# A masked softmax whose first half tile is loaded as two transfers, 16 partitions and 112

## The chip, the core and the metric

The kernel runs on one core of a Trainium2 chip. The metric is device time in microseconds (us) of one execution; lower is better. Engines are named as in the profile: DVE is VectorE, ACT is ScalarE, POOL is GpSimd, PE is TensorE, and SP is SyncE, which here only issues transfers.

## What is computed

A softmax over the last axis, of which only the first `lengths[b]` columns count; the other columns of the output are zero.

```python
x: (16, 8, 256, 256) float32;  lengths: 16 whole numbers from 128 to 255
for b in range(batch):
    masked = x[b, :, :, :lengths[b]]
    masked = masked - np.max(masked, axis=-1, keepdims=True)
    exp_masked = np.exp(masked)
    result[b, :, :, :lengths[b]] = exp_masked / np.sum(exp_masked, axis=-1, keepdims=True)
```

## The kernel before, in words

One batch is 2048 rows of 256 numbers, 2 MB. It is laid on 128 partitions with 16 rows each (`nt` = 16), so a partition holds 16 KB of a batch, and half a tile (`half` = 8 rows a partition) is 1 MB, or 8 KB a partition. Eight such tiles (`slots`) lie in the on-chip buffer `xt`. The 16 batches go through them in the order that `batch_of` gives; the first is batch 1.

For each batch: a load; a mask on VectorE (`mask`, `clip`, L248), which pulls the columns past the length far down; the exponential on ScalarE, as one instruction for the first four rows of a partition (L374) and one for each further row with its sum taken along (L377); on VectorE the sum of the first four rows (`total`, L269), then for each half a reciprocal (L279) and a multiplication (`divide`, L282); a store. The largest element is not subtracted. A check at the end (L317 to L328) finds whether any sum left the safe range, and only then a second, safe version runs.

Loads come from three queues. ScalarE's queue loads the lengths (L142). SP's queue loads the first tile in two halves (L145), each with a semaphore of its own, `s_ld[0]` and `s_ld[1]`:

```python
for h in range(2):
    s = slice(h * half, (h + 1) * half)
    nc.sync.dma_start(out=xt[:, 0, s], in_=x_f[batch_of(0), :, s]).then_inc(s_ld[h], 16)
```

POOL's queue loads the next three tiles whole (L196), after it has filled part of a later slot with zeros and has waited for `s_v`; the remaining twelve are loaded in a loop (L168), each only as wide as its length needs, in steps of 8 columns from 160, and each after an earlier load has landed and an earlier store has freed the slot.

Behind its two loads SP issues all stores (L154), in pieces of a quarter tile to a whole one (`parts`). Each waits for the multiplication that made its data (`s_out`), and up to the thirteenth tile also for the store two tiles before (L153).

VectorE masks the first tile in two halves. `mask(0, first half)` waits until `s_ld[0]` is 16, `mask(0, second half)` until `s_ld[1]` is 16. Every other mask treats a whole tile. After these two, VectorE's order is written out by hand: divide the first half, mask the next tile, divide the second half, sum the next tile's first rows.

Of the kernel before, what the change touches and what calls it, by code (L numbers as in the profile page):

```python
# [21 lines left out]
def kernel(  # L22
# [6 lines left out]
    nc = tc.nc  # L29
    P = nc.NUM_PARTITIONS  # L30
# [5 lines left out]
    half = nt // 2  # L36
# [3 lines left out]
    x_f = x.rearrange("b h q k -> b (h q) k").rearrange("b (p t) k -> b p t k", p=P)  # L40
# [9 lines left out]
    def batch_of(pos):  # L50
        return pos + 1 if pos < ahead - 1 else {ahead - 1: 15, 15: 0}.get(pos, pos)
# [22 lines left out]
    xt = pool.tile([P, slots, nt, seq_k], F32, name="xt")  # L74
# [31 lines left out]
    with tc.tile_critical(no_gpsimd_drain=True):  # L106
# [4 lines left out]
        s_ld = [sem(f"s_ld{k}") for k in range(3)]  # L111
# [28 lines left out]


        nc.scalar.dma_start(out=word64, in_=lengths[None, :]).then_inc(s_word, 16)  # L142
        for h in range(2):
            s = slice(h * half, (h + 1) * half)
            nc.sync.dma_start(out=xt[:, 0, s], in_=x_f[batch_of(0), :, s]).then_inc(s_ld[h], 16)  # L145
        for b in range(batch):
            s_b = s_st[b % 2] if b < late else s_late if b < batch - 1 else s_last
            for s in parts(b):
# [3 lines left out]
                if 2 <= b < late and s.start == 0:  # L152
                    nc.sync.wait_ge(s_b, 64 * (b // 2 + 2))  # L153
                nc.sync.dma_start(  # L154
                    out=out_f[batch_of(b), :, s, :], in_=xt[:, b % slots, s, :]
# [67 lines left out]
        def step(ins):  # L223
# [8 lines left out]
                out=down, in0=iota_i, scalar1=0.5, scalar2=-big, op0=ALU.add, op1=ALU.mult  # L232
# [7 lines left out]
                out=len_s, in0=len_f, scalar1=big, scalar2=None, op0=ALU.mult  # L240
# [4 lines left out]
        def clip(b, s, lo, hi):  # L245

            t = xt[:, b % slots, s, lo:hi]
            return nc.vector.scalar_tensor_tensor(  # L248
                out=t,
                in0=down[:, None, lo:hi].to_broadcast([P, s.stop - s.start, hi - lo]),  # L250
                scalar=len_s[:, batch_of(b) : batch_of(b) + 1],
                in1=t,
                op0=ALU.add,
                op1=ALU.min,
            )

        def mask(b, s):
            if b == 0:
                nc.vector.wait_ge(s_ld[s.start // half], 16)
            elif b == ahead - 1:  # L260
                nc.vector.wait_ge(s_ld[2], 16)
            else:
                par = (b - 1 if b < ahead else b) % 2
                nc.vector.wait_ge(s_sw[par], 16 * max(b // 2, 1))
            clip(b, s, mid, seq_k).then_inc(s_min, 1)
# [10 lines left out]
        def divide(b, h):  # L276
# [10 lines left out]
            ).then_inc(s_out, 1)  # L287

        mask(0, slice(0, half))
        mask(0, slice(half, nt))  # L290
        total(0)
        for b in range(batch):


            first = b != 1
            if first:
                divide(b, 0)
            if b + 1 < batch:
                mask(b + 1, slice(0, nt))
            if not first:  # L300
                divide(b, 0)
            divide(b, 1)
            if b + 1 < batch:
                total(b + 1)
# [14 lines left out]
        for k, (_, _, edge, op) in enumerate(checks):  # L319
            nc.vector.tensor_scalar(  # L320
                out=bad[:, k : k + 1],
# [13 lines left out]
        with nc.vector.Else():  # L335
            with nc.Fori(0, batch, 1, engines=[DVE]) as i:
                nc.vector.wait_ge(g_ld, 16 * i + 16)
                nc.vector.scalar_tensor_tensor(
                    out=g_t,
# [8 lines left out]
                    out=neg_max, in_=g_t, op=ALU.max, axis=AX, negate=True  # L348
# [5 lines left out]
                    out=g_t,  # L354
# [10 lines left out]
        with nc.Fori(0, batch // slots, 1, engines=[ACT]) as turn:  # L365
            for slot in range(slots):
                for h in range(2):
# [7 lines left out]
                    for j in range(h * half + lump * (1 - h), (h + 1) * half):  # L375
                        e = xt[:, slot, j, :]
                        ins = nc.scalar.activation(  # L377
                            out=e, in_=e, func=EXP, accum_out=row_sum[:, slot, j : j + 1]
# [5 lines left out]
        with nc.scalar.If(a_redo >= 1):  # L384
# [4 lines left out]
            with nc.Fori(0, batch, 1, engines=[ACT]) as i:  # L389
                nc.scalar.dma_start(out=g_t, in_=x_g[:, bass.ds(i, 1)]).then_inc(g_ld, 16)  # L390
                nc.scalar.wait_ge(g_v, 3 * i + 2)
                with nc.Fori(0, nt, 1, engines=[ACT]) as t:
                    e = g_t[:, bass.ds(t, 1), :]
                    nc.scalar.activation(
                        out=e,
                        in_=e,
# [41 lines left out]
```

## Time and profile before

| What | Value |
|---|---|
| Time, median of 3 runs (lowest to highest) | 154.69 us (154.58 to 154.70) |
| Span of the profiled execution, first to last instruction | 152.8 us |
| VectorE busy | 134.6 us |
| ScalarE busy | 95.1 us |
| GpSimd busy | 21.3 us |
| Read from and written to main memory | 27.98 MB and 33.55 MB |
| Mean rate of all transfers over the span | 403 GB/s |
| First-half and second-half load, issue to landing (median of the two) | 6.4 us |

How to read it: the profile is of one execution and its span is a little shorter than the time of a run, which also covers what lies before the first and after the last instruction. A window row gives, for a stretch of the span, the length, then busy time and number of instructions of PE, PEld, DVE, ACT and POOL, the clock granted to TensorE, the mean busy share of the 16 DMA engines and their GB/s. A packet is counted in the stretch in which it starts, with its whole length and duration, so a share can pass 1. A timeline row gives start, duration, engine, line, operation, tiles, and in brackets how long the engine was idle before and who released it; "SPq" and "POOLq" are issues of transfers.

### The profile page before, as it was taken

The numbers are of one execution on the slowest core, as the hardware profiler recorded it, in microseconds if no ns is written. First come the engines' busy times: TensorE is split into PE (matmuls) and PEld (weight loads), VectorE is DVE, ScalarE is ACT, GpSimd is POOL, SyncE is SP. The second block draws the span as 40 slices with busy tenths as digits, with TensorE's granted clock in tenths as the row PEclk, the third lists the DMA queues.
The fourth block names the chain that finished last, engine by engine and source line by source line (L and its number), as shares of the span: only waits on it lengthen the run. The fifth ranks groups of instructions, "written<-read, shape, count | busy, mean of one in ns | idle before, by whom it ended". The sixth has DMA issues, their size and how long they took to land.

```text
span 152.8 us, 818 instructions
## 1 busy us (share of the span) xinstructions
PE 0.3 (0%) x2; PEld 0.2 (0%) x2; DVE 134.6 (88%) x107; ACT 95.1 (62%) x402; POOL 21.3 (14%) x29
## 2 busy tenths in 40 slices
PE   0000000000000000000000000000000000000000
PEld 0000000000000000000000000000000000000000
DVE  1369999999999999999999999999999999999500
ACT  3096699339394967859393939577593939395000
POOL 4962110030303020030300220302000000000000
DMA  4999999999999999999999999999999999999994
GB/s 107 420 446 433 401 435 347 421 445 420 394 397 422 405 421 411 411 409 405 419 411 418 408 399 419 408 410 423 417 421 419 413 420 422 435 435 442 429 410 187
DMA packets 10646, 61.57 MB, mean 403 GB/s; under 512 B 898, under 2 KB 1010, under 8 KB 7058
## 3 DMA queue, kind: packets, MB, share of 16 engines
q1 hardware_dynamic: 5904, 35.65, 56.7%
q0 software_dynamic: 4736, 25.89, 41.9%
q14 instruction: 4, 0.03, 0.1%
q10 hardware_dynamic: 2, 0.00, 0.0%
HBM read 27.98 MB, written 33.55 MB: 403 GB/s over the span
## 4 chain that ended last, share of the span: by engine, by line
DVE 87%; DMA 5%; issue 1%; SPq 0%; PE 0%
DVE xt L282 48%; DVE xt L248 23%; DVE row_sum L269 12%; DMA xt<-in_x_dram 5%; DVE inv_sum L279 3%; DVE ends L317 0%; SPq L145 0%; DVE bad L320 0%; PE count L218 0%; DVE redo L328 0%; SPq L433 0%; SPq L106 0%
## 5 line engine op out<-in xcount | busy, mean ns | idle before, releaser
L377 ACT ACTIVATE xt<-xt 128x256 f32<-128x256 f32 x192 | 76.6, 400 | 0.2 <-DVE xt L248 0.2
L282 DVE TENSOR_TENSOR xt<-xt,inv_sum 128x2048 f32<-128x2048 f32 x32 | 73.3, 2292 | 1.1
L374 ACT ACTIVATE xt<-xt 128x1024 f32<-128x1024 f32 x16 | 16.9, 1056 | 42.8 <-DVE xt L248 42.8
L248 DVE SCALAR_TENSOR_TENSOR xt<-down,len_s,xt 128x2048 f32<-128x2048 f32 (+1 forms) x17 | 37.7, 2219 | 5.0 <-DMA xt<-in_x_dram 5.0
L377 ACT ACTIVATION_READ_ACCUMULATOR xt<-xt 128x1 f32 x192 | 35.9, 187 | 0.0
L168 POOL DMA_DIRECT2D xt<-in_x_dram x12 | 13.2, 1104 | 84.0 <-DMA xt<-in_x_dram 62.3
L269 DVE TENSOR_REDUCE row_sum<-xt 128x4 f32<-128x1024 f32 x16 | 19.4, 1210 | 0.0
L279 DVE RECIPROCAL inv_sum<-row_sum 128x8 f32<-128x8 f32 x32 | 6.3, 198 | 0.5
L191 POOL MEMSET xt<- 128x1536 f32 x4 | 5.4, 1398 | 1.1 <-DVE len_s L239 1.1
L361 ACT ACT_TABLE_LOAD x1 | 1.3, 1283 | 1.6 <-SPq L106 1.6
L196 POOL DMA_DIRECT2D xt<-in_x_dram x3 | 1.8, 590 | 0.0
L231 DVE TENSOR_SCALAR down<-iota_i 128x256 f32<-128x256 int32 x1 | 0.3, 300 | 1.6 <-POOL iota_i L181 1.6
L317 DVE TENSOR_REDUCE ends<-inv_sum 128x1 f32<-128x256 f32 x2 | 0.7, 408 | 0.0
L236 DVE CAST len_b<-word 1x16 bf16<-1x16 int32 x1 | 0.2, 164 | 0.4 <-DMA word<-in_lengths_dram 0.4
L239 DVE TENSOR_SCALAR len_s<-len_f 128x16 f32<-128x16 f32 x1 | 0.2, 176 | 0.3 <-PE len_f L216 0.3
L218 PE MATMUL count<-bad,ones_c 128*1 128x3 bf16 x1 | 0.2, 165 | 140.8 <-DVE bad L320 140.8
L181 POOL IOTA iota_i<- 128x256 int32 x1 | 0.3, 331 | 0.6 <-SPq L106 0.6
L328 DVE TENSOR_REDUCE redo<-count 1x1 f32<-1x3 f32 x1 | 0.1, 150 | 0.3 <-PE count L218 0.3
L320 DVE TENSOR_SCALAR bad<-ends 128x1 bf16<-128x1 f32 x3 | 0.3, 150 | 0.0
L187 POOL MEMSET seed<- 1x1 f32 x2 | 0.2, 225 | 0.0
L218 PEld LDWEIGHTS count<-bad,ones_c 128*1 128x1 bf16 x1 | 0.1, 79 | 140.8 <-DVE bad L320 140.8
L361 ACT ACTIVATE warm<-const-float32-0.0 128x1 f32<-128x1 f32 x1 | 0.2, 204 | 0.0
(10 smaller groups left out, 1.1 us busy)
## 6 DMA issues: line engine op xcount, KB each, us to landing
out_dram<-xt SPq DMA_DIRECT2D x20, 1024.0 KB
xt<-in_x_dram POOLq DMA_DIRECT2D x4, 2048.0 KB, 16.3
out_dram<-xt SPq DMA_DIRECT2D x15, 512.0 KB
xt<-in_x_dram POOLq DMA_DIRECT2D x3, 1728.0 KB, 16.7
out_dram<-xt SPq DMA_DIRECT2D x2, 2048.0 KB
xt<-in_x_dram POOLq DMA_DIRECT2D x2, 1600.0 KB, 16.0
xt<-in_x_dram POOLq DMA_DIRECT2D x2, 1280.0 KB, 14.7
xt<-in_x_dram SPq DMA_DIRECT2D x2, 1024.0 KB, 6.4
```

Source lines behind the costliest of these rows:

```text
L168: nc.gpsimd.dma_start(out=xt[:, slot, :, :w], in_=x_n[:, b, :, :w]).then_inc(s_sw[par], 16)
L191: nc.gpsimd.memset(xt[:, b, :, low:], 0.0).then_inc(s_fill, 1)
L196: nc.gpsimd.dma_start(out=xt[:, b], in_=x_f[batch_of(b)]).then_inc(s_sw[b - 1] if b < 3 else s_ld[2], 16)
L218: nc.tensor.matmul(count, lhsT=ones_c, rhs=bad, start=True, stop=True).then_inc(s_count, 1)
L248: return nc.vector.scalar_tensor_tensor(out=t, in0=down[:, None, lo:hi].to_broadcast([P, s.stop - s.start, hi - lo]), scalar=len_s[:, batc ...
L269: nc.vector.tensor_reduce(out=row_sum[:, b % slots, :lump], in_=xt[:, b % slots, :lump, :], op=ALU.add, axis=AX,).then_inc(s_exp[0], 1)
L279: step(nc.vector.reciprocal(out=inv_sum[:, b, s], in_=row_sum[:, b % slots, s]))
L282: nc.vector.tensor_tensor(out=t, in0=t, in1=inv_sum[:, b, s, None].to_broadcast([P, half, seq_k]), op=ALU.mult,).then_inc(s_out, 1)
L317: step(nc.vector.tensor_reduce(out=ends[:, k : k + 1], in_=values, op=op, axis=AX))
L361: nc.scalar.activation(out=warm, in_=nc.const_aps.tensor(0.0, (P, 1), F32), func=EXP)
L374: nc.scalar.activation(out=e, in_=e, func=EXP).then_inc(s_lump, 1)
L377: ins = nc.scalar.activation(out=e, in_=e, func=EXP, accum_out=row_sum[:, slot, j : j + 1])
```

## The change

The first half of the first tile is loaded as two transfers on SP's queue, one after the other: partitions 0 to 15, then partitions 16 to 127. The second half is still one transfer of all partitions, now the third on the queue. Both pieces of the first half count on `s_ld[0]`, and the first mask waits until it is 32. All lines below move down by one.

```diff
-        for h in range(2):
+        edge = 16
+        for h, p in ((0, slice(0, edge)), (0, slice(edge, P)), (1, slice(0, P))):
             s = slice(h * half, (h + 1) * half)
-            nc.sync.dma_start(out=xt[:, 0, s], in_=x_f[batch_of(0), :, s]).then_inc(s_ld[h], 16)
+            nc.sync.dma_start(out=xt[p, 0, s], in_=x_f[batch_of(0), p, s]).then_inc(s_ld[h], 16)
...
             if b == 0:
-                nc.vector.wait_ge(s_ld[s.start // half], 16)
+                nc.vector.wait_ge(s_ld[s.start // half], 16 * (2 - s.start // half))
```

## The prediction

> **What bounds the kernel now.** I read the page's head and its slices first, then the chain that ended last, then the timeline at both ends, then busy time by window.
>
> ```profile
> span 152.8 us, 818 instructions
> PE 0.3 (0%) x2; PEld 0.2 (0%) x2; DVE 134.6 (88%) x107; ACT 95.1 (62%) x402; POOL 21.3 (14%) x29
> ...
> DMA  4999999999999999999999999999999999999994
> GB/s 107 420 446 433 401 435 347 421 445 420 394 397 422 405 421 411 411 409 405 419 411 418 408 399 419 408 410 423 417 421 419 413 420 422 435 435 442 429 410 187
> ...
> DVE 87%; DMA 5%; issue 1%; SPq 0%; PE 0%
> ```
>
> Two things look full: VectorE (DVE, 88%) and the 16 DMA engines (a 9 in every slice but the first and last). The chain names VectorE for 87%. It is followed back from the last instruction of an engine, though, and stores still run after that. The end of the timeline and the windows around it decide:
>
> ```profile
> 142.46 0.36 SPq L154 DMA_DIRECT2D out_dram<-xt  x1
> ...
> 143.74 0.15 DVE L328 TENSOR_REDUCE redo<-count 1x1 f32<-1x3 f32 x1 [0.26 <-PE count L218]
> ```
> ```profile
> 10.00:20.00 10.00, 0.00 (x0) 0.00 (x0) 9.90 (x9) 7.20 (x33) 1.84 (x3) 1.00 1.02 427
> 20.00:24.00 4.00, 0.00 (x0) 0.00 (x0) 3.96 (x4) 4.00 (x16) 0.03 (x1) 1.00 0.92 370
> 24.00:60.00 36.00, 0.00 (x0) 0.00 (x0) 35.55 (x27) 23.37 (x101) 4.63 (x4) 1.00 1.02 413
> 60.00:100.00 40.00, 0.00 (x0) 0.00 (x0) 39.52 (x29) 27.60 (x122) 5.76 (x5) 1.00 1.02 410
> 100.00:140.00 40.00, 0.00 (x0) 0.00 (x0) 39.48 (x31) 29.23 (x125) 1.15 (x1) 1.00 1.02 422
> ...
> 142.50:150.00 7.50, 0.17 (x1) 0.08 (x1) 1.10 (x7) 0.00 (x0) 0.00 (x0) 1.00 0.98 418
> 150.00:152.80 2.80, 0.00 (x0) 0.00 (x0) 0.00 (x0) 0.00 (x0) 0.00 (x0) 1.00 0.26 108
> ```
>
> The last two columns are the mean busy share of the DMA engines and GB/s. The last store is issued at 142.46 and VectorE is through at 143.89, yet 418 x 7.5 + 108 x 2.8 = 3.4 MB still go out after 142.5. The last store is only 1 MB of that: the engines have a backlog of over 2 MB, and have been at a share of about 1.0 since 10 us. So the end is set by the DMA engines: when they start, how fast they are in the first microseconds, and then 61 MB at their pace. VectorE is some 7 us ahead at the end. A gap in the engines at the start is not made up later; one in VectorE is.
>
> The start, in detail:
>
> ```profile
> 1.14 0.86 SPq L145 DMA_DIRECT2D xt<-in_x_dram  x2
> ...
> 4.37 1.76 POOL L196 DMA_DIRECT2D xt<-in_x_dram  x3
> ...
> 6.46 1.28 DVE L248 SCALAR_TENSOR_TENSOR xt<-down,len_s,xt 128x1024 f32<-128x1024 f32 x1 [3.47 <-DMA xt<-in_x_dram]
> ...
> 9.26 1.29 DVE L248 SCALAR_TENSOR_TENSOR xt<-down,len_s,xt 128x1024 f32<-128x1024 f32 x1 [1.52 <-DMA xt<-in_x_dram]
> ...
> 14.27 10.95 SPq L154 DMA_DIRECT2D out_dram<-xt  x5
> ```
> ```profile
> 0.00:2.00 2.00, 0.00 (x0) 0.00 (x0) 0.30 (x1) 0.35 (x1) 0.92 (x10) 1.00 0.00 0
> 2.00:3.00 1.00, 0.17 (x1) 0.10 (x1) 0.34 (x2) 0.99 (x2) 0.00 (x0) 1.00 0.95 172
> 3.00:4.00 1.00, 0.00 (x0) 0.00 (x0) 0.00 (x0) 0.14 (x1) 0.95 (x1) 1.00 0.91 319
> 4.00:5.00 1.00, 0.00 (x0) 0.00 (x0) 0.00 (x0) 0.00 (x0) 1.00 (x2) 1.00 0.95 401
> 5.00:6.00 1.00, 0.00 (x0) 0.00 (x0) 0.00 (x0) 0.00 (x0) 1.00 (x3) 1.00 1.00 418
> ```
>
> Nothing moves before 2 us. Against the 427 GB/s of 10 to 20 us, the three microseconds from 2 to 5 lose (255 + 108 + 26) / 427 = 0.91 us. That is the most that a better start could give back.
>
> **The change, part by part.** It adds one transfer on SP's queue, and cuts the first 1 MB (128 rows of 8 KB) into 16 rows and 112 rows. Of compute instructions nothing is added or moved; the first mask waits for both pieces on one semaphore.
>
> *One more issue on SP.* Two issues take 0.86 us, so 0.43 each. The 112 rows are issued 0.43 later than the whole was begun, at about 1.57, and the second half at about 2.0 instead of 1.57. The second half hides: the engines need 8 packets each of the first half before it, and that work lasts beyond 5 us. Behind it on SP stands the first store, which is issued at 14.27 because it waits for VectorE. POOL's loads (4.37) and ScalarE's load of the lengths stand on other queues, and neither is moved. Cost 0; if that cover were gone, 0.43.
>
> *The first packets.* Two windows give the price of one 8 KB packet on one engine:
>
> ```profile
> DMA packets 14, 0.11 MB, mean 209 GB/s; under 512 B 0, under 2 KB 0, under 8 KB 0
> ...
> q1 hardware_dynamic: 14, 0.11, 136.1%
> ```
> ```profile
> DMA packets 24, 0.20 MB, mean 393 GB/s; under 512 B 0, under 2 KB 0, under 8 KB 0
> ...
> q1 hardware_dynamic: 24, 0.20, 92.7%
> ```
>
> The first window is 2.05 to 2.6 us: 1.361 x 16 engines x 0.55 us / 14 packets = 0.86 us each. The second is 4.6 to 5.1: 0.927 x 16 x 0.5 / 24 = 0.309 us each. The engines do not start together:
>
> ```profile
> 2.00:2.20 0.20, 0.00 (x0) 0.00 (x0) 0.00 (x0) 0.20 (x1) 0.00 (x0) 1.00 0.68 123
> 2.20:2.40 0.20, 0.00 (x0) 0.00 (x0) 0.09 (x1) 0.20 (x1) 0.00 (x0) 1.00 2.41 328
> 2.40:2.60 0.20, 0.00 (x0) 0.01 (x1) 0.07 (x1) 0.20 (x1) 0.00 (x0) 1.00 0.66 123
> 2.60:2.80 0.20, 0.17 (x1) 0.09 (x1) 0.00 (x0) 0.20 (x1) 0.00 (x0) 1.00 0.35 123
> ```
>
> GB/s x 0.2 us / 8.192 KB counts the packets that start in each row: 3, 8, 3 and 3. So 16 engines take up their first packet over some 0.6 us, on average near 2.35. If the spread is the time in which 128 rows are described, 16 rows are described in an eighth of it, all engines start near 2.2, and their next packets (issued at 1.57, so due 0.43 after the present times, 2.6 to 3.2) are there when a 0.86 us packet ends. That gives 2.35 - 2.2 = 0.15 us per engine, 0.55 for the last engine; if the spread has another cause, nothing. I take 0.15.
>
> *Where these packets write.* In the present load the 16 engines work at the same time on rows spread over all 128 partitions. In the first piece all 16 first packets go to 16 neighbouring partitions, and come from one stretch of x. No row of the trace has such a transfer. If the engines then share their way into the memory by n, each first packet has (n - 1) x 0.309 more: 0 for n = 1, 0.31 for two, 0.93 for four, 2.2 for eight, and 15 x 0.309 = 4.6 us for all sixteen, which is the far end. The nearest row (24 packets at 0.309 each, 128 partitions) is n = 1; but it owes that pace to its spread, and a sixteenth of the partitions at no loss would mean that any place takes the pace of all 16. I take the middle of the five steps, n = 4: +0.93.
>
> The Trainium skill, "SBUF — State Buffer", section "Door 1: The DMA port swizzle", speaks against the change: partitions 0 to 15 reach 4 of the 16 DMA ports, and a transfer to them was measured there at 104 GB/s. By that page 128 KB would take 1.26 us instead of the 0.31 of a full-width packet, an estimate of +0.95, and the sum would come out the same; no run here shows it yet.
>
> *The 112 rows.* Each engine has 7 rows instead of 8. If shares are neighbouring rows, 7 do not line up with the 8 that each engine has in every other transfer, so now and then two engines meet in one place, in the 112 rows and where a late engine still writes them while the next transfer begins. Nothing in the trace shows it: 0 if they never meet, two packets (0.62) if a quarter of the seven meet another's; I take 0.2, nearer to the row of undisturbed packets.
>
> *After that.* VectorE's first two masks start after waits on these loads (6.46 and 9.26), so its whole row shifts by about the same 1 us. That is covered by its 7 us at the end. The thinnest place of the DMA row is 20 to 24 (share 0.92); stores come 1 us later there, but loads are queued, so I cost it at 0. If that cover fails it costs up to the same 1 us once more.
>
> **Sum:** 0.93 - 0.15 + 0.2 = +0.98, say +1.0 us. The profiled span is 152.8; the median of the runs, 154.69, is 1.9 above it, for what lies around the span. So a span of 153.8, and 152.8 + 1.0 + 1.9 = **155.7 us**. With two sharing it is 0.31 - 0.15 + 0.2 = +0.4, with four, the full 0.62 and nothing won at the start +1.55: the forecast's own range is 155.1 to 156.3.
>
> **The rivals.**
>
> *Faster: the engines start together.* No sharing (n = 1), shares that do not meet, and the spread of first packets is gone. For it: 0.6 us of spread, first packets of 0.86 us that would cover the gap to the second issue, and an end set by the last engine. It decides if the last engine to start is also the last to end: 0.15 on average, 0.55 for the last, in the middle 0.35: 154.3 us. Against it: 16 engines on 16 partitions must cost nothing.
>
> *No change.* The first data come when the memory answers, whenever a packet is taken up: the early packets take 0.86 us and so end together with later ones. Then starting earlier only lengthens the first packet: 154.7. This is also the case in which the change does not do what it says. The Trainium skill, "DMA: Bandwidth & Descriptors", section "Rules for kernel authors", says of two transfers to disjoint partition halves "Don't bother", since both spray over the same 16 engines; that would be this rival, and the full DMA row agrees that there is no free engine to win.
>
> *Slower by another way: engines belong to partitions.* If an engine serves fixed rows, 16 rows wake only two to four engines and the others wait for the second issue, 0.43 later than now. No packet is slowed, but most engines start 0.43 later, and with an end set by the last one that is +0.43: 155.1. The same page, section "Why a DMA increments its semaphore by 16 and not by 1", has 16 and 112 rows both split over 16 engines, which speaks against it; no run here shows it.
>
> **How the numbers follow.** Chances: the forecast 0.55, engines by partition 0.13, no change 0.14, start together 0.18. Something within 0.2% (0.31 us) is about what a measurement of this kernel cannot tell from no change. Faster by more: 0.14 of the rival's 0.18 and nothing else. Within: the 0.14 of no change, the rival's other 0.04, and 0.04 of engines by partition, 0.22. Slower: 0.55 and 0.09, 0.64. The range leaves out the far sharing (eight or sixteen, about 0.1) above and the largest gain below: 154.3 to 156.3.
>
> **What would show it.** In the changed profile SP has three issues of 0.43, about 1.3 us together. If the engines start together, all 16 first packets start before 2.4. If they share, packets that start before 2.6 take 1.2 us or more rather than 0.86, the rows from 2 to 5 lose about 1.9 us instead of 0.91, the first mask starts near 7.4 and the second near 10.2, and the tail after 142.5 is longer by 1 us while rows from 24 to 140 keep 410 to 422 GB/s. If engines belong to partitions, few packets start before 2.6 and each takes no longer. The forecast is wrong if the first packets take 0.9 us or less, or if the loss at the start grows and the end does not follow, which would mean that the end is not set by the DMA engines.

## The result

The changed kernel takes 155.62 us (median of 10 runs) against 154.61 for the kernel before (10 runs): 1.0071 times, interval 1.0052 to 1.0090. It is slower by 1.0 us (1.1 by the ratio), as forecast, and 155.62 stands beside the forecast of 155.7. The profile and the runs below say that two of the forecast's terms had the wrong size, though, and that their errors cancelled: the number was met by luck.

The profiled execution of the changed kernel took 156.72 us, 1.1 above the median, so a second profile (155.74 us, span 154.1) is drawn on below wherever the size matters. First the head of the page, after:

```profile
span 155.1 us, 819 instructions
...
DMA  4999999999999999999999999999999999999991
GB/s 91 285 431 444 427 424 382 417 434 427 397 390 423 407 417 415 414 411 401 417 414 412 410 408 415 409 410 421 418 423 417 419 419 425 427 444 439 408 429 59
```

At the start the first two slices differ most (91 and 285 GB/s where there were 107 and 420); the last one is lower too (59 where there was 187). The windows of the start, after; the last two columns are the DMA engines' busy share and GB/s:

```profile
2.00:2.20 0.20, 0.00 (x0) 0.00 (x0) 0.00 (x0) 0.20 (x1) 0.00 (x0) 1.00 0.45 164
2.20:2.40 0.20, 0.00 (x0) 0.00 (x0) 0.10 (x1) 0.20 (x1) 0.00 (x0) 1.00 1.86 492
2.40:2.60 0.20, 0.00 (x0) 0.02 (x1) 0.06 (x1) 0.20 (x1) 0.00 (x0) 1.00 0.02 0
```
```profile
2.00:3.00 1.00, 0.17 (x1) 0.10 (x1) 0.34 (x2) 0.99 (x2) 0.00 (x0) 1.00 1.28 238
3.00:4.00 1.00, 0.00 (x0) 0.00 (x0) 0.00 (x0) 0.14 (x1) 0.95 (x1) 1.00 0.60 156
4.00:5.00 1.00, 0.00 (x0) 0.00 (x0) 0.00 (x0) 0.00 (x0) 1.00 (x2) 1.00 0.91 328
5.00:6.00 1.00, 0.00 (x0) 0.00 (x0) 0.00 (x0) 0.00 (x0) 1.00 (x3) 1.00 1.02 295
6.00:7.00 1.00, 0.00 (x0) 0.00 (x0) 0.00 (x0) 0.00 (x0) 1.00 (x2) 1.00 1.04 246
7.00:8.00 1.00, 0.00 (x0) 0.00 (x0) 0.00 (x0) 0.00 (x0) 1.00 (x2) 1.00 0.93 295
```

164 x 0.2 / 8.192 = 4 packets start before 2.2 us and 12 before 2.4: all 16 engines have begun, sooner than before. Then no packet of 8 KB starts for 0.2 us. From 4 to 8 the engines are nearly always busy (0.91 to 1.04) but move only 246 to 328 GB/s, where before they moved 401 to 475. So packets do not wait there; they take longer. Share x 16 us / packets gives 0.36 us a packet in the row from 4 to 5 and 0.41 to 0.56 in the three behind it, instead of 0.309. All of these packets are still on SP's queue. The first 1 MB is through near 6.1 us by the sum of the rows, so the slow packets last into the second half, which is loaded at full width.

The price of the first packets themselves, and of those behind them, after, from 2.05 to 2.4 us and from 2.6 to 3.0:

```profile
DMA packets 16, 0.13 MB, mean 374 GB/s; under 512 B 0, under 2 KB 0, under 8 KB 0
...
q1 hardware_dynamic: 16, 0.13, 132.0%
```
```profile
DMA packets 21, 0.11 MB, mean 266 GB/s; under 512 B 8, under 2 KB 8, under 8 KB 8
...
q1 hardware_dynamic: 21, 0.11, 202.8%
```

The narrow piece's 16 packets take 1.320 x 16 x 0.35 / 16 = 0.46 us each (0.51 in the second profile). The 13 packets of the 112 rows behind them take 2.028 x 16 x 0.4 / 13 = 1.0 us each.

A measure for all kernels here is the time lost from 2 to 8 us: the sum of (427 - GB/s) / 427 over its six rows. Before it is 0.80 us; after, 2.35, and 2.20 in the second profile. That is 1.4 to 1.55 more, of which 1.0 is in the median time. Of the first profile's 1.55, only 0.40 falls from 2 to 5 us, where the forecast had it, and 1.15 from 5 to 8.

The rest of the run, after:

```profile
1.14 1.33 SPq L146 DMA_DIRECT2D xt<-in_x_dram  x3
...
8.52 1.28 DVE L249 SCALAR_TENSOR_TENSOR xt<-down,len_s,xt 128x1024 f32<-128x1024 f32 x1 [5.53 <-DMA xt<-in_x_dram]
12.48 1.28 DVE L249 SCALAR_TENSOR_TENSOR xt<-down,len_s,xt 128x1024 f32<-128x1024 f32 x1 [2.67 <-DMA xt<-in_x_dram]
```
```profile
24.00:60.00 36.00, 0.00 (x0) 0.00 (x0) 35.55 (x27) 24.95 (x108) 4.63 (x4) 1.00 1.01 410
60.00:100.00 40.00, 0.00 (x0) 0.00 (x0) 39.48 (x30) 28.20 (x120) 4.80 (x5) 1.00 1.02 411
100.00:140.00 40.00, 0.00 (x0) 0.00 (x0) 39.55 (x29) 27.25 (x116) 2.10 (x2) 1.00 1.02 423
```
```profile
143.38 2.29 DVE L283 TENSOR_TENSOR xt<-xt,inv_sum 128x2048 f32<-128x2048 f32 x1
```

Three issues of 0.44; the second mask starts 3.2 us later than before (12.48 against 9.26) and VectorE's last multiplication ends 3.2 later (145.67 against 142.44). The time grew by 1.0 only. The transfer rows from 24 to 140 are the same as before, within 3 GB/s.

### The profile page after: what moved, and what is told of

It is laid out like the page before. It is cut to its first block, busy times and chain, and to the rows that moved or that the text cites. A ratio compares the mean times of both kernels' runs of the same rounds, so it can differ in the third digit from the quotient of the medians.

```text
span 155.1 us, 819 instructions
## 1 busy us (share of the span) xinstructions
PE 0.3 (0%) x2; PEld 0.2 (0%) x2; DVE 134.7 (87%) x107; ACT 95.1 (61%) x402; POOL 21.3 (14%) x29
## 4 chain that ended last, share of the span: by engine, by line
DVE 86%; DMA 7%; issue 1%; SPq 1%; PE 0%
DVE xt L283 47%; DVE xt L249 23%; DVE row_sum L270 12%; DMA xt<-in_x_dram 7%; DVE inv_sum L280 3%; SPq L146 1%; DVE ends L318 0%; DVE bad L321 0%; PE count L219 0%; DVE redo L329 0%; SPq L434 0%; SPq L106 0%
```

## The experiments

Three theories at first: **A**, the forecast's, that the narrow piece is itself slow; **B**, that the 112 rows are, as their shares do not line up; **C**, that any third transfer at the start costs its issue. All ratios are to the kernel before, and a difference in us is its ratio's excess over 1 times the 154.6 us of that kernel; by this measure the change is +1.1.

**An extra narrow load ahead of two whole halves.** Edit:

```diff
+        nc.sync.dma_start(out=extra[0:16], in_=x_f[batch_of(0), 0:16, :half]).then_inc(s_extra, 16)
         for h in range(2):
```

> The kernel before, with one more load ahead of its first half: the same 16 rows of 8 KB as the change's first piece, to partitions 0 to 15 of a buffer that nothing reads. The two half loads stay whole. In every theory the 16 packets take 0.31 us of each engine. Theory A (the narrow piece is itself slow, four engines to a way): 0.31 + 0.93 - 0.15 = +1.1 us against before. Theory B (the 112 rows are what is slow, because their shares do not line up): +0.2 to +0.4. Theory C (a third transfer at the start costs its issue, whatever it holds): 0.31 + 0.43 = +0.7.

Measured: 155.08 us, 1.0031 (1.0019 to 1.0043), so +0.48, of which 0.31 are the bytes that it adds. Net +0.17: A's 0.93 is refuted and C's +0.7 is just outside the interval (+0.29 to +0.66), which B's +0.2 to +0.4 overlaps. Its transfers in the window from 2.05 to 2.4 us, and from 2.5 to 3.0:

```profile
DMA packets 16, 0.13 MB, mean 374 GB/s; under 512 B 0, under 2 KB 0, under 8 KB 0
...
q1 hardware_dynamic: 16, 0.13, 103.6%
```
```profile
DMA packets 30, 0.11 MB, mean 230 GB/s; under 512 B 16, under 2 KB 16, under 8 KB 16
...
q1 hardware_dynamic: 30, 0.11, 151.9%
```

The 16 packets take 1.036 x 16 x 0.35 / 16 = 0.36 us each, far from four times 0.309. But the 14 packets of the load behind them (the other 16 of these 30 are the 4-byte ends of the narrow load) take 1.519 x 16 x 0.5 / 14 = 0.87 us: the slow first packet of the kernel before (0.86) is still there, one transfer later. The early start of all engines is won and lost again.

**The same 16 rows, to every eighth partition.**

```diff
-        nc.sync.dma_start(out=extra[0:16], in_=x_f[batch_of(0), 0:16, :half]).then_inc(s_extra, 16)
+        nc.sync.dma_start(out=extra[0:128:8], in_=x_f[batch_of(0), 0:16, :half]).then_inc(s_extra, 16)
```

> As the kernel with the extra narrow load, but its 16 rows go to partitions 0, 8, 16 up to 120 instead of 0 to 15; source, bytes and number of packets are the same. Theory A: engines share less, +0.2 to +0.6, clearly below the narrow one. Theory B and theory C: the same as the narrow one (+0.2 to +0.4, and +0.7).

Measured: 155.53 us, 1.0067 (1.0053 to 1.0080), +1.0. Slower than the narrow one, which no theory had. The issue of that load on SP, in the narrow and then in the spread kernel:

```profile
1.14 0.39 SPq L145 DMA_DIRECT2D extra<-in_x_dram  x1
```
```profile
1.14 0.61 SPq L145 DMA_DIRECT2D extra<-in_x_dram  x1
```

In the profile the spread load's issue takes 0.61 instead of 0.39, and 131 GB/s instead of 246 start between 2 and 3 us. The late start hides the comparison that was wanted, so this run decides nothing on A; the pair of eight loads below does.

**Cut by rows instead of partitions.**

```diff
-        for h in range(2):
-            s = slice(h * half, (h + 1) * half)
+        for h, s in ((0, slice(0, 1)), (0, slice(1, half)), (1, slice(half, nt))):
```

> The first half is again loaded as two transfers, an eighth and seven eighths of its bytes, but both take all 128 partitions: row 0 of each partition, then rows 1 to 7. Theory A: no narrow piece and no shares that do not line up, so -0.2 to +0.2. Theory B: the same. Theory C: as slow as the change, +0.5 to +1.0.

Measured: 154.80 us, 1.0010 (0.9996 to 1.0025), +0.15. A third issue and a small first piece cost little or nothing while every transfer is 128 partitions wide. C is out.

**Cut at 64.**

```diff
-        edge = 16
+        edge = 64
```

> The change with its cut at partition 64 instead of 16: two pieces of 64 rows, 4 rows to each engine in both. Theory A as a theory of shared ways: both pieces are half as wide as the memory, so if two engines share each way all the time the 1 MB takes twice its 2.47 us, +2 to +2.5. Theory B in its narrow form (only shares that do not line up cost): 4 is a half of 8, so they line up and it costs +0.2 or less. Theory C: as the change, +1.0.

Measured: 156.74 us, 1.0139 (1.0123 to 1.0154), +2.1. The windows of its start:

```profile
4.00:5.00 1.00, 0.00 (x0) 0.00 (x0) 0.00 (x0) 0.00 (x0) 1.00 (x2) 1.00 1.04 221
5.00:6.00 1.00, 0.00 (x0) 0.00 (x0) 0.00 (x0) 0.00 (x0) 1.00 (x3) 1.00 1.16 262
6.00:7.00 1.00, 0.00 (x0) 0.00 (x0) 0.00 (x0) 0.00 (x0) 1.00 (x2) 1.00 0.88 180
7.00:8.00 1.00, 0.00 (x0) 0.00 (x0) 0.00 (x0) 0.00 (x0) 1.00 (x2) 1.00 1.04 213
```

From 4 to 8 us the mean is 219 GB/s at full busy share, half of 427: two engines to a way, as A's general idea has it, and B in its narrow form (4 lines up with 8) is refuted. The Trainium skill, "SBUF — State Buffer", section "Door 1: The DMA port swizzle", has 64 partitions reach 8 of 16 ports, at 196 GB/s; the trace agrees, with 219.

So the theories were formed anew. **S**: engines share the places of the on-chip buffer, all the time that a transfer is narrow or its shares meet others'; only the lone first piece escapes. **G**: the gap behind the small first piece is what costs.

**The pieces in the other order.**

```diff
-        for h, p in ((0, slice(0, edge)), (0, slice(edge, P)), (1, slice(0, P))):
+        for h, p in ((0, slice(edge, P)), (0, slice(0, edge)), (1, slice(0, P))):
```

> The change with its two pieces in the other order: partitions 16 to 127 first, then 0 to 15, then the second half. Theory S (engines that write rows of the same places at the same time share them, and the 112 rows make them meet; the lone 16 rows at the very start escape, since the next load's start covers them): +0.6 to +1.1, about as slow as the change, with packets over 0.35 us from about 3 to 8 us. Theory G (what costs is the gap between a small first piece and the start of the next load, which the small piece can't cover): the gap is gone, +0 to +0.3.

Measured: 156.26 us, 1.0107 (1.0092 to 1.0121), +1.65. Its rows from 6 to 8 us:

```profile
6.00:7.00 1.00, 0.00 (x0) 0.00 (x0) 0.00 (x0) 0.00 (x0) 1.00 (x2) 1.00 0.89 148
7.00:8.00 1.00, 0.00 (x0) 0.00 (x0) 0.00 (x0) 0.00 (x0) 1.00 (x2) 1.00 1.01 221
```

With no small piece in front, and so no gap behind one, it is slower than the change. G is refuted, and S was too low (+0.6 to +1.1). That the 16 rows no longer escape when they stand behind 112 would explain it, but no run shows that it is these rows that cost the time.

**An extra load of 112 rows, and of 128, ahead of two whole halves.**

```diff
+        nc.sync.dma_start(out=extra[16:128], in_=x_f[batch_of(0), 16:128, :half]).then_inc(s_extra, 16)
...
+        nc.sync.dma_start(out=extra[0:128], in_=x_f[batch_of(0), 0:128, :half]).then_inc(s_extra, 16)
```

> The kernel before, with an extra load of 112 rows of 8 KB (partitions 16 to 127 of a buffer that nothing reads) ahead of its two whole half loads. 7 packets of 0.309 are 2.16 us. Theory S: 2.16 + 0.5 to 1.0, that is as slow as or slower than the same with 128 rows. Theory G: 2.16 + 0.1, so 0.3 less than with 128 rows.

> As the kernel with the extra 112 rows, but with 128 rows: 8 packets of 0.309 on each engine. Both theories: +2.47. Where the end is set by the DMA engines, all of it is in the time, although VectorE has 7 us to spare; if VectorE's lead could hide it, it would be near 0.

Measured: 159.00 us with 112 rows, 1.0289 (1.0259 to 1.0318), +4.5; 157.75 with 128, 1.0203 (1.0187 to 1.0219), +3.1. The load with fewer bytes costs 1.25 us more. The start with 112 rows, and then with 128:

```profile
4.00:5.00 1.00, 0.00 (x0) 0.00 (x0) 0.00 (x0) 0.00 (x0) 1.00 (x2) 1.00 1.02 254
5.00:6.00 1.00, 0.00 (x0) 0.00 (x0) 0.00 (x0) 0.00 (x0) 1.00 (x2) 1.00 1.10 279
6.00:7.00 1.00, 0.00 (x0) 0.00 (x0) 0.00 (x0) 0.00 (x0) 1.00 (x3) 1.00 0.91 238
```
```profile
4.00:5.00 1.00, 0.00 (x0) 0.00 (x0) 0.00 (x0) 0.00 (x0) 1.00 (x2) 1.00 1.00 426
5.00:6.00 1.00, 0.00 (x0) 0.00 (x0) 0.00 (x0) 0.00 (x0) 1.00 (x3) 1.00 1.03 434
6.00:7.00 1.00, 0.00 (x0) 0.00 (x0) 0.00 (x0) 0.00 (x0) 1.00 (x2) 1.00 1.00 426
```

This is the change's own row pattern, without any 16-row piece. With 112 rows the rate is 238 to 279 GB/s. The 112 rows are 0.92 MB and by the rows through before 6 us, so the row from 6 to 7 is mostly of the full-width load that follows; with 128 rows the rate is full. G wanted the 112 rows to be 0.3 cheaper, and is refuted once more; S has the direction. Both kernels are slower than the sums had it (+2.47 for 128 rows), for a reason of their own: in both VectorE becomes the bound. With 128 extra rows, a stretch near the end in which the transfer engines run out of work, and the last multiplication:

```profile
140.00:145.00 5.00, 0.00 (x0) 0.00 (x0) 4.93 (x5) 3.60 (x14) 0.00 (x0) 1.00 0.77 331
```
```profile
147.65 2.29 DVE L286 TENSOR_TENSOR xt<-xt,inv_sum 128x2048 f32<-128x2048 f32 x1
```

It ends at 149.94, 6.4 us before the end of a span of 156.3; in the kernel before it ends 10.4 before (142.44 of 152.8). In the five kernels in which VectorE is through latest (these two and the three that follow) that rest is 6.3 to 6.8 us and no less. So the stores behind VectorE need about 6.4 us, and its slack before was about 4.0 us and not 7. The 1.25 us between the two kernels go through VectorE's waits, so they are no direct measure of the transfers; the rows above are.

**The first half in eight pieces of 16 neighbours.**

```diff
-        for h, p in ((0, slice(0, edge)), (0, slice(edge, P)), (1, slice(0, P))):
+        for h, p in [(0, slice(i, i + edge)) for i in range(0, P, edge)] + [(1, slice(0, P))]:
```

> The first half is loaded as eight pieces of 16 neighbouring partitions, so that each engine has one row of each, and every piece is as narrow as the change's first. The pieces are issued over 8 x 0.43 = 3.4 us. Theory S with four engines to a place: the 1 MB takes four times its 2.47 us, +6 to +7.5. If a narrow piece is as quick as the lone one was (0.37 us a packet): bound by the issues, +1.0 to +1.5.

Measured: 160.90 us, 1.0411 (1.0398 to 1.0425), +6.35. Two windows of its start and its transfers from 4 to 7 us:

```profile
4.00:5.00 1.00, 0.00 (x0) 0.00 (x0) 0.00 (x0) 0.00 (x0) 1.00 (x2) 1.00 1.05 131
5.00:6.00 1.00, 0.00 (x0) 0.00 (x0) 0.00 (x0) 0.00 (x0) 1.00 (x3) 1.00 1.05 131
```
```profile
DMA packets 96, 0.39 MB, mean 131 GB/s; under 512 B 48, under 2 KB 48, under 8 KB 48
...
q1 hardware_dynamic: 96, 0.39, 105.4%
```

1.054 x 16 x 3 / 48 = 1.05 us for a packet of 8 KB (the piece's 48 small end packets counted in), 3.4 times 0.309, at a steady 131 GB/s. Narrow pieces in a row are as slow as the forecast had feared of one. The Trainium skill, "SBUF — State Buffer", section "Door 1: The DMA port swizzle", has 104 GB/s for partitions 0 to 15; the direction agrees, and the 131 measured here decides.

**Where is it shared?** Neighbouring partitions also come from neighbouring rows of x. Two kernels with eight extra loads of 16 rows take this apart, one with only the destination narrow, one with only the source:

```diff
+        for i in range(8):
+            nc.sync.dma_start(
+                out=extra[16 * i : 16 * i + 16], in_=x_f[batch_of(0), i:128:8, :half]
+            ).then_inc(s_extra, 16)
...
+                out=extra[i:128:8], in_=x_f[batch_of(0), 16 * i : 16 * i + 16, :half]
```

> The kernel before, with eight extra loads of 16 rows ahead of its two half loads, to a buffer that nothing reads. Each goes to 16 neighbouring partitions, but its rows come from all over the batch (every eighth of 128). Question: what an 8 KB packet takes once the stream runs (0.309 in a full-width load, 1.02 in the kernel with eight pieces of 16 rows). Theory S (engines share places of the on-chip buffer): about 1.0 again, 131 GB/s. Theory M (the rows of a piece lie side by side in main memory, and that is what is shared): near 0.31 to 0.5, bound by the issues at 0.43 each, some 300 GB/s. The whole run is 6 to 10 us slower than before by S, 3 to 4 by M.

> The other way round: eight extra loads of 16 rows that lie side by side in main memory, each to every eighth partition (0, 8, 16 up to 120, and so on). Theory S: less sharing than with 16 neighbours, packets of 0.31 to 0.65, 200 to 400 GB/s. Theory M: about 1.0, 131 GB/s.

Measured, one run each beside 154.92 of the kernel before: 167.77 and 171.11 us. The whole times are no measure here, as both are far beyond VectorE's slack. The packets are; the narrow destination from 4 to 7 us, then the narrow source from 3.1 to 5.4 us:

```profile
DMA packets 104, 0.43 MB, mean 142 GB/s; under 512 B 52, under 2 KB 52, under 8 KB 52
...
q1 hardware_dynamic: 104, 0.43, 102.7%
```
```profile
DMA packets 112, 0.49 MB, mean 214 GB/s; under 512 B 52, under 2 KB 52, under 8 KB 52
...
q1 hardware_dynamic: 112, 0.49, 71.5%
```

A narrow destination: 1.027 x 16 x 3 / 52 = 0.95 us a packet, 142 GB/s, engines always busy. A narrow source: 0.715 x 16 x 2.3 / 60 = 0.44 us, and the engines idle for over a quarter of the time, as each issue takes 0.63 us. So a narrow destination alone makes the packets about three times as long, and a narrow source alone still lets 214 GB/s through: for 16-row pieces it is the on-chip side that is shared. What makes 0.44 out of 0.309 with the spread destination, no run here tells.

**The change once more,** with no edit, for a second profile.

> The changed kernel once more, for a second profile: the first one is of an execution of 156.72 us, 1.1 above the median. In every theory the first piece's 16 packets start within 0.2 us of each other and are through before 3 us, the rows from 4 to 8 us are well under 400 GB/s, and the second mask starts near 12. If the 1.1 us come from one engine that is late by itself, the span is near 154.0 here and the rate from 2 to 8 us is about the same as in the first profile.

Measured: 155.74 us, span 154.1. Four windows of it:

```profile
4.00:5.00 1.00, 0.00 (x0) 0.00 (x0) 0.00 (x0) 0.00 (x0) 1.00 (x2) 1.00 1.08 360
5.00:6.00 1.00, 0.00 (x0) 0.00 (x0) 0.00 (x0) 0.00 (x0) 1.00 (x3) 1.00 0.96 246
6.00:7.00 1.00, 0.00 (x0) 0.00 (x0) 0.00 (x0) 0.00 (x0) 1.00 (x2) 1.00 1.03 279
7.00:8.00 1.00, 0.00 (x0) 0.00 (x0) 0.00 (x0) 0.00 (x0) 1.00 (x2) 1.00 0.94 352
```

The same picture: busy engines, 246 to 360 GB/s. Nearly the same time is lost by 8 us as in the first profile (2.20 against 2.35) while the span is 1.0 shorter, so that execution's extra microsecond came later. The ends of the two show where; the first profile, then the second:

```profile
152.00:153.00 1.00, 0.00 (x0) 0.00 (x0) 0.00 (x0) 0.00 (x0) 0.00 (x0) 1.00 0.08 33
153.00:154.00 1.00, 0.00 (x0) 0.00 (x0) 0.00 (x0) 0.00 (x0) 0.00 (x0) 1.00 0.02 8
```
```profile
152.00:153.00 1.00, 0.00 (x0) 0.00 (x0) 0.00 (x0) 0.00 (x0) 0.00 (x0) 1.00 0.04 16
```

33 + 8 GB/s for a microsecond each are 5 packets of 8 KB, and the trace has them one behind the other from 152.1 to 153.6. With 0.08 x 16 = 1.3 us of work in the first of these rows it is in effect one engine that ends alone. In the second profile the last packet ends at 152.6. So the extra microsecond is one late engine, the case that the expectation names; why it was late stays open.

The lost time goes with the times of all kernels that VectorE does not bound. Lost from 2 to 8 us above the 0.80 of before, plus the extra load's own 0.31 where there is one, beside the measured difference:

| Kernel | lost more | extra bytes | sum, us | measured, us |
|---|---|---|---|---|
| cut by rows | 0.40 | 0 | 0.40 | 0.15 |
| extra narrow load | 0.31 | 0.31 | 0.62 | 0.48 |
| extra spread load | 0.73 | 0.31 | 1.04 | 1.04 |
| the change (two profiles) | 1.40, 1.55 | 0 | 1.40, 1.55 | 1.1 |
| other order | 1.86 | 0 | 1.86 | 1.65 |
| cut at 64 | 2.28 | 0 | 2.28 | 2.15 |

The order is that of the times, and most of the loss is in the time; up to 0.5 us is given back. One place where that happens stands in the rows: from 20 to 24 us the transfers before ran at 370 GB/s (share 0.92) and lost 4 x (427 - 370) / 427 = 0.53 us, and in the changed kernel they lose next to nothing there:

```profile
20.00:24.00 4.00, 0.00 (x0) 0.00 (x0) 4.00 (x3) 4.00 (x18) 0.54 (x1) 1.00 1.00 423
```

## Why the prediction was right, point by point

**The bound: right, with a wrong margin.** The end follows the DMA engines' start: see the table, and VectorE, which slipped by 3.2 us, not the 1 of the forecast, while the time grew by 1.0. The forecast read VectorE's 7 us of lead off the span; the stores behind it take part of that, and the true slack was about 4.0 us. By these numbers a second mask that slipped by over 5 us would have made VectorE set the end (an estimate: 4.0 of slack and 1.0 of longer time). The thin place from 20 to 24, which the forecast costed at 0 and feared as a loss, gave back up to 0.5 us.

**One more issue on SP: right.** Three issues of 0.44, and with pieces of full width +0.15, an interval that includes no change.

**The engines start together: right, but it wins nothing.** All 16 packets start by 2.4. The step that failed is that the next packets are there "when a 0.86 us packet ends". The first packets took 0.46 us in the change and 0.36 with the extra narrow load, no packet of 8 KB started from 2.4 to 2.6 us, and the next load's first packets took 1.0 and 0.87 us, the long first packet that the narrow ones had not had.

**The narrow first piece, n = 4, +0.93: wrong by most of its size.** The forecast named first packets of 0.9 us or less as a sign against itself, and they took 0.46. Alone at the start the narrow load costs +0.17 (0.48 - 0.31), with what the common start won counted in. The sharing itself is real, 3.4 times a packet in a row of such pieces, and on the on-chip side. That the lone piece escapes because its rows are written while the next load has not yet brought data fits the 0.2 us without a new packet and the slower result of the other order, but is only argued.

**The 112 rows, +0.2: too small by a factor of four to five.** What the change costs beyond the lone narrow piece is 1.1 - 0.17 = 0.93 us by the ratios (0.8 by the medians). It is a remainder, as no run has the 112 rows alone in the first half. That 112 rows are slow, the extra load of them shows: 238 to 279 GB/s where 128 rows get 426 to 434. The forecast gave a reason for a loss here, shares of 7 that do not line up with 8, but chose the value near undisturbed packets, and let it reach only the beginning of the next transfer; the rows from 6 to 8 us show it well into that full-width load. That the reason is the 7 is not shown: all pieces of 112 rows here begin at partition 16, and no run has another number of rows near 128, or the same number from partition 0. The sum of 0.98 was right by luck, because 0.93 - 0.15 and 0.2 stood where 0.17 and 0.93 belong.

**The rivals.** Faster through a common start: refuted, since the start was had and not the time. No change: refuted. Engines by partition: refuted, as the first piece's 16 packets all start by 2.4, the 112 rows' first ones do not start before 2.6, and 16 end packets follow the same load in the run with the extra narrow load. The Trainium skill, "DMA: Bandwidth & Descriptors", section "Rules for kernel authors", says "Don't bother" of two transfers to disjoint halves because they share the engines anyway; the runs show more than that, a loss of 2.1 us at 64 and 64.

## What to carry to other kernels

Where the DMA engines are full from start to end, a load that takes part of the partitions can cost more than its bytes: pieces of 16 rows in a row, of 64 and of 112 all did here, and behind 112 rows the full-width transfer was slowed too. Where a first load must be cut, cut it by rows of each partition (+0.15 here) rather than by partitions (+1.1 to +6.35); a cut by columns was not tried. And compare rates window by window: in these traces a busy share near 1.0 at half the GB/s meant longer packets, and a share below 1.0 engines without work.

## What was not expected of the hardware

- 112 rows load more slowly than 128: 238 to 279 against 426 to 434 GB/s in the same three microseconds, and +4.5 against +3.1 us of time.
- The first packets of a load at the start take 0.86 us and not 0.309, and this does not go with being the first transfer: 16 rows ahead of it took 0.36 each, and the load behind them 0.87.
- The issue of a load to every eighth partition took 0.61 us on SP against 0.39 for 16 neighbours. In the kernel cut at 64 the issues were as long, and nothing here tells why.
